# The exponential of the routing weights moved behind the key look-ups and behind a GELU; the turned keys copied by VectorE

## The chip, the cores and the metric

The kernel runs on one core of a Trainium2 chip. The metric is the time of one execution on the device, in microseconds (us). Five engines work side by side, each through its own queue, in the order of that queue: TensorE (PE in the profile; its weight loads are PEld), VectorE (DVE), ScalarE (ACT), GpSimd (POOL) and SyncE (SP, which here issues the loads). They meet only through waits that the program's builder puts on instructions.

## What is computed

A transformer forward pass over 256 tokens of width 1024, in float32: a first block (pooling, dilated attention, gates), and a second one with a convolution mixer and an attention mixer, each followed by an expert layer. The change is in the expert layer, which runs twice:

```python
def _peer(xn, w_q, subkeys, u_tab, v_tab):
    q = (t @ w_q).reshape(n_tok, PEER_HEADS, 2, SUB_DIM)           # 8 heads, 2 halves of a key
    sc = jnp.einsum("thpd,hpnd->thpn", q, subkeys)
    sv, si = lax.top_k(sc, PEER_TOPK)                              # the 16 best of 128 subkeys
    cand = sv[:, :, 0, :, None] + sv[:, :, 1, None, :]
    cidx = si[:, :, 0, :, None] * N_KEYS + si[:, :, 1, None, :]
    top_v, pos = lax.top_k(cand, PEER_TOPK)                        # the 16 best pairs
    idx = jnp.take_along_axis(cidx, pos, axis=-1)
    g = jax.nn.softmax(top_v, axis=-1)                             # the routing weights
    ...
    a = g * gelu(einsum(x, u_tab[idx]))
    out = einsum(a, v_tab[idx])
```

There are 128 x 128 experts. The kernel doesn't gather: it multiplies all tokens by all of U (128 tiles of 128 experts), takes the GELU, multiplies by the routing weights laid out over all experts, and multiplies by all of V.

## The kernel before

`peer` streams U tile by tile. For each of 128 tiles `i`: the tile comes by DMA in four buffers (L102); it is split into two parts of lower precision whose sum is exact, `hi` by ScalarE (L121) and `lo` by VectorE or GpSimd (L122; up to tile 41 always GpSimd), with three tiles in parts at a time; TensorE makes 24 products of it (L132 to L134) into one of two PSUM banks; ScalarE reads that bank with a GELU into `X` (L1138; L1134 for the tokens whose weights are there already). The bank is free for the tile after the next one only when its GELU is done.

Beside that the routing runs, cut into 36 jobs, traced over the first J1 = 40 tiles (job k ahead of tile k * 40 // 36). Four jobs end the lists of best subkeys (`lists`, L960 to L974). Then, for each half `a` of the tokens (128 each): `candidates` and `best` (L993 to L1015, the best 16 pairs of a head), one job with `ranks` (L1017 to L1039) and `weights` (L1055 to L1067), four `keys` jobs (L1041 to L1053: the subkeys at these ranks, each L1046, L1051, L1053), and `turn` (L1069 to L1078: three transposes on TensorE into one PSUM bank, of the two keys and the weights; then copies to SBUF as `ij` and, in two parts, `gt`). `weights` is the softmax: subtraction of the largest (L1058, VectorE), exponential (L1060, ScalarE), sum, reciprocal, scale and product (L1062 to L1065, VectorE). For the first half `ranks` and `weights` fall ahead of tile 15 and `turn` ahead of tile 21; for the second half ahead of tiles 33 and 38. From tile 40 on `scatter` (L1080 to L1104) lays the weights of four tokens at a time over all experts: VectorE makes `o` (L1084) and two `wi` (L1089) from `ij` and `gt`, TensorE multiplies them into `G` (L1094).

Most tiles of the routing (`g`, `tv`, `key0`, `key1`, `e`, `ra`, `rb`) have one buffer, which the second half's jobs take over from the first's: the second half's `key0` and `g` can be written when the first half's transposes have read theirs.

The order of each engine's queue isn't that of the text. A planner in the builder goes through the program with times of its own for each instruction; whenever an engine is free in its plan, it takes the earliest traced of those instructions whose inputs are there. The splits are raised in that order (`AHEAD`). What it fixed, the chip runs, whatever its real times. ScalarE's functions come in sets: the exponential and the GELU each need a table load (ACT_TABLE_LOAD) when the other was loaded; the casts and copies need none.

Of the kernel before, what the change touches and what calls it, by code (L numbers as in the profile page):

```python
# [22 lines left out]
# The tokens stand in the order of (t % 4, t // 4 % 4, t // 16), in which a query's keys of the  # L23
# dilations 4 and 16 lie in its own half.
ORDER = np.arange(T).reshape(16, 4, 4).transpose(2, 1, 0).reshape(T)
# a head of two in a tile, its half of the partitions, and the other half
# [4 lines left out]
G_SCALE = 16384.0      # the routing weights' two float16 parts carry float32's significand  # L31
# how far ahead of their place in the program: splits of streamed weights, of kept ones, the norms
AHEAD, KEEP, CHAIN = 200, 100, 4000
HL = 3                 # streamed tiles in two parts at a time
WARM = 14              # products that start TensorE's clock while the first tokens load
RELIEF = 3             # splits behind a norm that leave VectorE to it
# peer: the tiles of U over which the routing ends and over which its weights are scattered, the
# tiles of V whose products for the second tokens come last, the tiles of X in its first part
# [12 lines left out]
def two_blocks(ctx: ExitStack, tc: tile.TileContext, io, out):  # L51
# [10 lines left out]
    def as_ordered(ap):  # L62
        """[128, T] in the sequence's order, read or written in ORDER's, and the other way round."""
        return ap.rearrange("p (c i j) -> p j i c", i=4, j=4)
# [26 lines left out]
    count, relief, fetched, pin, pinned = [0], [0], [0], [None], [0]  # L91

    more = []

    def fetch(src):
        """One tile on its way; where a phase has more room, every third in that."""
        fetched[0] += 1
        if more and fetched[0] % 3 == 1:
            raw = more[-1].tile([P, D], F32, tag="more", name="more")
        else:  # L100
            raw = stream.tile([P, D], F32, tag="raw", name="raw", bufs=4)
        SY.dma_start(out=raw, in_=src)  # L102
        return raw
# [21 lines left out]
    def in_order(dst, src):  # L125
        """A load behind the ones that stand before it: it may have to wait for its place."""
        tc.keep_in_program_order(SY.dma_start(out=dst, in_=src))
# [8 lines left out]
    def dense_t(src, acts, pool_share=0):  # L136
        """[128 columns of W, 256 tokens] of (tokens @ W), in PSUM; src: [128, 8, 128]."""
# [7 lines left out]
    def stacked(ps, dst):  # L145
        """Two heads' queries, over 8, in two parts: each head's first part in its half of the
        partitions, and its second in the other half."""
# [9 lines left out]
    def keeper(pool, src):  # L157
        """keep(i): W's rows 128 i.. in their two parts, read once for both token tiles."""
# [11 lines left out]
    def rows_kept(act_of, keep, nxt):  # L170
        """x += the sum over 8 tiles of act[:, a]^T @ W's 128 rows: all of the first token tile, then
        all of the second beside the first one's next norm."""
# [19 lines left out]
    def last_rows(nxt, acc0, acc1, steps, scale=None):  # L192
        """The second token tile's last products, one half after the other, and around them the
        way from the first one's sums into the next layer."""
# [38 lines left out]
    def sum_squares(a, half, k=0, of=None):  # L233
        """64 * mean(x * x), one half of it."""
# [4 lines left out]
    def mean_square(a):  # L239
        """64 * (mean(x * x) + eps)."""  # L240
# [5 lines left out]
    def inverse_root(a, m):  # L246
        """1 / sqrt(m / 64): Newton's steps r -> r * (3 - m * r * r) / 2, where each step's factor
        of 2 goes into the next step's m (64 * m, 16 * m, 4 * m)."""
# [14 lines left out]
    def spread(pool, src, tag="spread"):  # L263
        """A row of D parameters on all partitions."""
# [5 lines left out]
    class Enter:  # L270
        """The norm in front of a layer, and the products of the layer's first 512 columns, which run
        token tile by token tile: the first tile's while the second's sums are still open.
        take(a, sums [128 tokens, 512]); new(shape, type, name): a tile."""
# [32 lines left out]
        def both(self, a, r):  # L306
            """added and scaled in one."""
# [34 lines left out]
        def open(self):  # L342
            """Room for the products until the next layer has turned them."""
# [4 lines left out]
    class EnterConv(Enter):  # L348
        """Behind the first block: its closing norm and the convolution's, in one."""
# [18 lines left out]
        def inverse(self, a):  # L368
            """Of both norms: 1 / sqrt(mean(y * y) + eps * (mean(x * x) + eps)) with y = x * gain."""
# [13 lines left out]
    def turned(nat, n, which=p_tr):  # L383
        """n transposes of [128, 128], side by side in PSUM."""
# [8 lines left out]
    def split_act(pool, src, tag, bufs=1):  # L393
        """An SBUF tile [128, n] in two float32r parts."""
# [7 lines left out]
    def transpose_p(pool, pieces, name, bufs=None, which=p_acc):  # L402
        """Transposes of [128, 128] pieces, side by side."""
# [13 lines left out]
    # ------------------------------------------------------------------ first block  # L417
    def first_block(nxt):
        acts = xh, xl
        with ExitStack() as es:  # L420
# [66 lines left out]
            def window(g):  # L487
                """Windowed means minus the value."""
# [102 lines left out]
    def attention(acts, es1, at1, v_n, att, rest, loads):  # L591
        """Softmax over the keys of all three groups together."""
# [3 lines left out]
        # the first group's: per head a query's two parts, and over both the keys' first part  # L596
# [108 lines left out]
    # ------------------------------------------------------------------ second block  # L705
# [54 lines left out]
    def gqa_mixer(entered, nxt):  # L760
        acts, nat = (xh, xl), entered.nat
        with ExitStack() as es:
# [11 lines left out]
            def place_keys():  # L774
                """Each key head twice, over the queries' two parts."""
# [19 lines left out]
            def place(i):  # L795
                """Two heads of one key head: tile pair, partition half, tile, head."""
# [34 lines left out]
            def weighted(i, p_ts, pv):  # L831
                """Both key heads of a tile pair, each in its half of the partitions."""
# [91 lines left out]
    def peer(l, entered, nxt):  # L924
        acts, nat = (xh, xl), entered.nat
        with ExitStack() as es:
            with ExitStack() as es1:
# [8 lines left out]
                def xs(i):  # L936
                    return X[i >= XA][:, i % XA]
# [5 lines left out]
                # in the place of X's last parts  # L943
# [16 lines left out]
                def lists(n):  # L960
                    """The 16 best subkeys of one half of a head."""
# [79 lines left out]
                def keys(a, side, part):  # L1041
                    """The subkeys at these ranks, four heads at a time."""
# [12 lines left out]
                def weights(a):  # L1055
                    tv = state["tv"]
                    g = one.tile([P, 8, 16], F32, tag="g", name="g")
                    V.tensor_tensor(out=g, in0=tv, in1=tv[:, :, 0:1].to_broadcast([P, 8, 16]),  # L1058
                                    op=OP.subtract)
                    S.activation(out=g, in_=g, func=AF.Exp)  # L1060
# [6 lines left out]
                    state["g"] = g  # L1067

                def turn(a):  # L1069
# [5 lines left out]
                    S.copy(out=ij[:, :, s], in_=ps[:, 0:2 * P].rearrange("p (c t) -> p c t", c=2))  # L1075
# [4 lines left out]
                def scatter(tg, done):  # L1080
                    """The weights of four tokens over all experts, [key 1, token, key 0]."""
# [25 lines left out]
                for a in range(2):  # L1107
# [3 lines left out]
                    jobs.append(lambda a=a: (ranks(a), weights(a)))  # L1111
                    jobs += [lambda a=a, s=s, p=p: keys(a, s, p) for s in range(2) for p in range(2)]
                    jobs.append(lambda a=a: turn(a))
# [6 lines left out]
                for i in range(P):  # L1120
# [16 lines left out]
                    if ready < 64:  # L1137
                        S.activation(out=xs(i)[:, ready:], in_=ps[:, ready:], func=AF.Gelu)  # L1138
# [42 lines left out]
    class Finish:  # L1181
        """The closing norm, from the last sums."""
# [48 lines left out]
def _bucket(rel, n_buckets, max_distance):  # L1231
    """T5 bucket of a relative position (a constant of the shapes)."""
# [11 lines left out]
def _layout(a):  # L1244
    f = np.float32

    def cols(w, n0, n1):
        """Tiles of 128 columns: [tile, 128 rows, row block, 128]."""
# [6 lines left out]
    def rows(w):  # L1255
        """Tiles of 512 columns: [tile, 4, 128 rows, row block, 512]."""
# [76 lines left out]
```

## Time and profile before

| | |
|---|---|
| time of a run, median of 3 (lowest to highest) | 2212.44 us (2206.22 to 2213.91) |
| span of the profiled execution, first to last instruction | 2210.8 us |
| TensorE, products | busy 2152.8 us, 97%, 14288 instructions |
| TensorE, weight loads | 1961.3 us, 89% |
| VectorE | 1569.8 us, 71% |
| ScalarE | 1074.3 us, 49% |
| GpSimd | 353.3 us, 16% |
| DMA | 373.94 MB, mean 169 GB/s |

Of the profiled execution the span is what is listed; what lies around it is in the times of the runs alone. Busy shares are means over the whole span. A wait is put down to the engine whose instruction ended it last. Line numbers are those of the kernel before. The first GELU of U's tiles starts at 449.4 us in the first expert layer and at 1409.7 us in the second.

### The profile page before, as it was taken

What the parts mean: (1) busy time and instruction counts of PE and PEld (TensorE: products, weight loads), DVE (VectorE), ACT (ScalarE), POOL (GpSimd) and SP (SyncE); (2) the same over time, 40 slices, a digit from 0 to 9 for tenths busy, and PEclk for the clock granted to TensorE, in tenths of its full rate; (3) what the DMA queues carried; (4) which work ended last, traced back from release to release, by engine and by line L of the source; (5) the groups of instructions that cost most, each with busy time, mean ns of one, the idle gap of its engine ahead of it and who ended that gap; (6) DMA issues with size and microseconds to landing.
All of it is one profiled execution on the core that took longest, in us unless ns stands there. A gap on an engine that the chain in (4) does not pass through costs nothing. (4 is left out here: it accounts for less than half of the span.)

```text
span 2210.8 us, 37689 instructions
## 1 busy us (share of the span) xinstructions
PE 2152.8 (97%) x14288; PEld 1961.3 (89%) x14288; DVE 1569.8 (71%) x3045; ACT 1074.3 (49%) x1975; POOL 353.3 (16%) x167
## 2 busy tenths in 40 slices
PE   8999999998999999999999999989999999999998
PEld 7999988998999999888888767989999999888887
DVE  4456777798577898555666686994788896565665
ACT  4556544344444444444455574444444444444454
POOL 3310101378300000000000232687000000000000
PEclk9999999999999999999999999999999999999999
DMA  6635746345544444665656652545444446556664
GB/s 245 209 124 175 236 130 195 115 153 159 166 144 152 144 145 153 190 192 191 192 194 201 214 180 71 159 144 180 144 145 151 144 144 190 191 191 191 192 193 139
DMA packets 104437, 373.94 MB, mean 169 GB/s; under 512 B 12096, under 2 KB 14144, under 8 KB 103744
## 3 DMA queue, kind: packets, MB, share of 16 engines
q1 hardware_dynamic: 103968, 371.01, 52.3%
q8 instruction: 112, 1.84, 0.3%
q14 instruction: 69, 0.57, 0.1%
q10 hardware_dynamic: 288, 0.52, 0.1%
HBM read 370.44 MB, written 1.05 MB: 168 GB/s over the span
## 5 line engine op out<-in xcount | busy, mean ns | idle before, releaser
L132 PE MATMUL mm<-xh,hi 128*128 128x256 f32 x2880 | 834.7, 290 | 21.8 <-ACT xa L1138 21.4
L133 PE MATMUL mm<-xl,hi 128*128 128x256 f32 x2880 | 817.7, 284 | 0.0
L134 PE MATMUL mm<-xh,lo 128*128 128x256 f32 x2880 | 817.1, 284 | 0.4 <-POOL lo L122 0.4
L121 ACT CAST hi<-raw 128x1024 fp32r<-128x1024 f32 x600 | 632.0, 1054 | 299.0 <-issue 138.8
L122 DVE TENSOR_TENSOR lo<-raw,hi 128x1024 fp32r<-128x1024 f32 x484 | 591.7, 1223 | 222.4 <-ACT hi L121 217.7
L132 PEld LDWEIGHTS mm<-xh,hi 128*128 128x128 f32 x2880 | 556.7, 193 | 24.7 <-ACT xa L1138 22.2
L133 PEld LDWEIGHTS mm<-xl,hi 128*128 128x128 f32 x2880 | 556.0, 193 | 0.3
L134 PEld LDWEIGHTS mm<-xh,lo 128*128 128x128 f32 x2880 | 554.6, 193 | 1.0 <-POOL lo L122 0.8
L1159 PE MATMUL acc<-hi,al 128*128 128x512 f32 x976 | 384.5, 394 | 0.0
L1159 PE MATMUL acc<-lo,ah 128*128 128x512 f32 x976 | 382.6, 392 | 0.0
L1159 PE MATMUL acc<-hi,ah 128*128 128x512 f32 x976 | 378.7, 388 | 0.0
L122 POOL TENSOR_TENSOR lo<-raw,hi 128x1024 fp32r<-128x1024 f32 x118 | 307.7, 2619 | 248.3 <-ACT hi L121 239.0
L1159 PEld LDWEIGHTS acc<-lo,ah 128*128 128x128 f32 x976 | 183.2, 188 | 42.8
L1159 PEld LDWEIGHTS acc<-hi,ah 128*128 128x128 f32 x976 | 183.2, 188 | 40.9
L1159 PEld LDWEIGHTS acc<-hi,al 128*128 128x128 f32 x976 | 183.5, 188 | 36.4
L1151 ACT CAST ah<-xa 128x256 fp32r<-128x256 f32 x200 | 81.3, 407 | 271.8 <-PE acc L1159 271.0
L1152 DVE TENSOR_TENSOR al<-xa,ah 128x256 fp32r<-128x256 f32 x200 | 84.9, 425 | 111.2 <-ACT ah L1151 111.2
L294 POOL TENSOR_TENSOR enl<-raw,enh 128x1024 fp32r<-128x1024 f32 x5 | 12.4, 2487 | 850.9 <-ACT enh L293 850.9
L1094 PE MATMUL G<-wi,o 128*128 128x128 f16 x1024 | 142.9, 296 | 0.0
L1084 DVE TENSOR_TENSOR o<-iota,ij 128x1024 f16<-128x1024 f16 x128 | 94.4, 739 | 58.7 <-PE G L1094 58.1
L1104 ACT COPY xa<-G 128x240 f32<-128x240 f32 (+22 forms) x92 | 35.4, 385 | 200.3 <-DVE xa L1101 153.5
L1101 DVE TENSOR_TENSOR xa<-G,xa 128x400 f32<-128x400 f32 (+31 forms) x128 | 111.8, 873 | 11.0 <-PE G L1094 11.0
(461 smaller groups left out, 2190.6 us busy)
## 6 DMA issues: line engine op xcount, KB each, us to landing
raw<-in_peer_u_dram SPq DMA_DIRECT2D x256, 512.0 KB, 3.5
raw<-in_peer_v_dram SPq DMA_DIRECT2D x256, 512.0 KB, 3.5
raw<-in_peer_w_q_dram SPq DMA_DIRECT2D x24, 512.0 KB, 3.7
raw<-in_conv_w_in_dram SPq DMA_DIRECT2D x20, 512.0 KB, 4.4
raw<-in_w_rest_dram SPq DMA_DIRECT2D x18, 512.0 KB, 3.6
raw<-in_w_qk_dram SPq DMA_DIRECT2D x16, 512.0 KB, 4.2
more<-in_w_rest_dram SPq DMA_DIRECT2D x10, 512.0 KB, 3.6
raw<-in_w_v_dram SPq DMA_DIRECT2D x8, 512.0 KB, 4.6
```

What stands on the lines that cost most here:

```text
L121: S.copy(out=hi, in_=raw)
L122: (G if on_pool else V).tensor_tensor(out=lo, in0=raw, in1=hi.bitcast(F32), op=OP.subtract)
L132: PE.matmul(out=ps, lhsT=ah, rhs=bh, start=first and i == 0, stop=False)
L133: PE.matmul(out=ps, lhsT=ah, rhs=bl, start=False, stop=False)
L134: PE.matmul(out=ps, lhsT=al, rhs=bh, start=False, stop=last and i == n - 1)
L1084: V.tensor_tensor(out=o, in0=iota_4.unsqueeze(1).to_broadcast([P, 2, P, 4]), in1=ij[:, :, s].unsqueeze(2).to_broadcast([P, 2, P, 4]), op=O ...
L1094: PE.matmul(out=ps[:, t], lhsT=o[:, 1, :, t], rhs=wi[i][:, :, t], start=i == 0, stop=i == 1)
L1101: V.tensor_tensor(out=dst[:, :, :old], in0=ps[:, :, i0:i0 + old], in1=dst[:, :, :old], op=OP.mult)
L1104: S.copy(out=dst[:, :, old:], in_=ps[:, :, i0 + old:i0 + n])
L1151: S.copy(out=act[0], in_=src)
L1152: V.tensor_tensor(out=act[1], in0=src, in1=act[0].bitcast(F32), op=OP.subtract)
L1159: PE.matmul(out=acc[a][half], lhsT=p[:, s], rhs=r[:, d], start=i == 0 and w == 0, stop=i == P - 1 and w == 2)
```

## The change

The softmax is cut in three. `shifted` (the subtraction alone) is traced ahead of `ranks`, in the same job. A new job `exponentials` comes behind the four `keys` jobs; with `issue_after` the exponential gets a place in ScalarE's queue behind the last GELU traced before it (an order, not a wait). A further job holds the rest, `weights`; then `turn`. That makes 40 jobs for 40 tiles: for the first half `shifted` and `ranks` stand ahead of tile 14, the exponential ahead of tile 19, `weights` ahead of 20, `turn` ahead of 21; for the second half at 32, 37, 38 and 39. In `turn` the copy of the two turned keys goes from ScalarE to VectorE. The GELU's instruction is kept in `state["gelu"]`. The rest of the diff removes comments and changes no instruction.

```diff
-                def weights(a):
+                def shifted(a):
                     tv = state["tv"]
-                    g = one.tile([P, 8, 16], F32, tag="g", name="g")
-                    V.tensor_tensor(out=g, in0=tv, in1=tv[:, :, 0:1].to_broadcast([P, 8, 16]),
+                    state["g"] = one.tile([P, 8, 16], F32, tag="g", name="g")
+                    V.tensor_tensor(out=state["g"], in0=tv, in1=tv[:, :, 0:1].to_broadcast([P, 8, 16]),
                                     op=OP.subtract)
-                    S.activation(out=g, in_=g, func=AF.Exp)
+
+                def exponentials():
+                    with tc.issue_after(state["gelu"]):
+                        S.activation(out=state["g"], in_=state["g"], func=AF.Exp)
+
+                def weights():
+                    g = state["g"]
                     z = one.tile([P, 8], F32, tag="gz", name="gz")
...
-                    state["g"] = g
...
-                    S.copy(out=ij[:, :, s], in_=ps[:, 0:2 * P].rearrange("p (c t) -> p c t", c=2))
+                    V.tensor_copy(out=ij[:, :, s], in_=ps[:, 0:2 * P].rearrange("p (c t) -> p c t", c=2))
...
-                    jobs.append(lambda a=a: (ranks(a), weights(a)))
+                    jobs.append(lambda a=a: (shifted(a), ranks(a)))
                     jobs += [lambda a=a, s=s, p=p: keys(a, s, p) for s in range(2) for p in range(2)]
+                    jobs.append(exponentials)
+                    jobs.append(weights)
                     jobs.append(lambda a=a: turn(a))
...
                     if ready < 64:
-                        S.activation(out=xs(i)[:, ready:], in_=ps[:, ready:], func=AF.Gelu)
+                        state["gelu"] = S.activation(out=xs(i)[:, ready:], in_=ps[:, ready:],
+                                                     func=AF.Gelu).ins
```

## Rows read from the trace of the kernel before

**Rows 1.** TensorE's waits (total us, times, longest), and the timeline at one's end.
```profile
PE mm L132 <- ACT xa L1138: 21.4, 4, 9.2
...
471.84 0.58 PE L132 MATMUL mm<-xh,hi 128*128 128x256 f32 x1 [3.27 <-ACT xa L1138]
```

**Rows 2.** Waits of the other engines, the whole span.
```profile
DVE gt L1077 <- ACT ij L1075: 56.9, 2, 28.6
...
ACT g L1060 <- DVE g L1058: 22.2, 4, 9.4
```

**Rows 3.** ScalarE's timeline, first layer: start, duration, operation, [idle before, releaser].
```profile
507.58 0.37 ACT L1138 ACTIVATE xa<-mm 128x256 f32<-128x256 f32 x1
...
513.33 0.38 ACT L1138 ACTIVATE xa<-mm 128x256 f32<-128x256 f32 x1
...
513.99 1.28 ACT L1060 ACT_TABLE_LOAD   x1
521.17 0.31 ACT L1060 ACTIVATE g<-g 128x128 f32<-128x128 f32 x1 [5.90 <-DVE g L1058]
521.39 1.03 ACT L121 CAST hi<-raw 128x1024 fp32r<-128x1024 f32 x1
522.43 1.28 ACT L1138 ACT_TABLE_LOAD   x1
523.73 0.38 ACT L1138 ACTIVATE xa<-mm 128x256 f32<-128x256 f32 x1
```

**Rows 4.** Busy us of PE, PEld, DVE, ACT, POOL; PEclk, DMA, GB/s; after three stalls.
```profile
471.84:478.01 6.17, 6.17 (x29) 6.17 (x30) 6.17 (x7) 1.98 (x3) 4.41 (x2) 0.50 0.42 104
...
1432.08:1438.00 5.92, 5.92 (x49) 5.92 (x50) 5.92 (x4) 2.50 (x4) 5.92 (x3) 1.00 0.37 100
1486.04:1491.77 5.73, 5.73 (x27) 5.73 (x28) 5.73 (x5) 1.54 (x3) 4.99 (x2) 0.50 0.28 94
```

**Rows 5.** TensorE's timeline: the first half's transposes of the keys, both layers.
```profile
512.25 0.38 PE L1074 MATMUL tr<-ident,key 128*128 128x128 f32 x2
...
1470.61 0.38 PE L1074 MATMUL tr<-ident,key 128*128 128x128 f32 x2
```

**Rows 6.** VectorE's timeline, first layer, around the second half's first look-ups.
```profile
513.45 0.22 DVE L1023 TENSOR_SCALAR t<-pos 128x128 uint32<-128x128 uint32 x1
513.58 2.43 DVE L1025 TENSOR_SCALAR m__6335<-pos 128x128 f32<-128x128 uint32 x1
...
518.39 1.23 DVE L1051 TENSOR_TENSOR e<-e,sif 128x1024 bf16<-128x1024 bf16 x1
519.72 1.22 DVE L1053 TENSOR_REDUCE key<-e 128x64 f32<-128x1024 bf16 x1
520.86 0.28 DVE L1058 TENSOR_TENSOR g<-tv 128x128 f32<-128x128 f32 x1
```

**Rows 7.** VectorE's groups, 468.6 to 520 us: count, busy us, mean ns, idle before.
```profile
L1051 DVE TENSOR_TENSOR e<-e,sif 128x1024 bf16<-128x1024 bf16 x5 | 14.0, 2803 | 0.0
```

**Rows 8.** VectorE's timeline, second layer.
```profile
1437.52 2.38 DVE L1064 TENSOR_SCALAR gz<-gz 128x8 f32<-128x8 f32 x1
...
1440.08 2.50 DVE L1065 TENSOR_TENSOR g<-g,gz 128x128 f32<-128x128 f32 x1
...
1480.27 1.23 DVE L1051 TENSOR_TENSOR e<-e,sif 128x1024 bf16<-128x1024 bf16 x1
```

**Rows 9.** Timelines of TensorE and VectorE, first layer: second half's transposes to first scatter.
```profile
569.88 0.27 PE L1074 MATMUL tr<-ident,g 128*128 128x128 f32 x1
...
571.42 0.29 DVE L1077 CAST gt<-tr 128x128 f16<-128x128 f32 x1 [28.33 <-ACT ij L1075]
...
573.72 0.74 DVE L1089 TENSOR_TENSOR wi<-o,gt 128x512 f16<-128x512 f16 x2
...
575.76 0.41 PE L1094 MATMUL G<-wi,o 128*128 128x128 f16 x2
```

## Prediction

> **What bounds the kernel now.** I read the table of busy shares first: TensorE 97%, no other engine over 71%. So the time is TensorE's own work plus what it loses, and an edit on ScalarE or VectorE counts only where TensorE waits for it. The waits of TensorE come next. By far the largest is "mm <- ACT xa L1138", 21.4 us in 4 waits, two in each layer [rows 1]: a product finds its PSUM bank still unread, because the GELU that reads it is late. The first wait of each layer takes 3.3 us (one is shown), the second layer's other one 9.2, which leaves 5.7 for the first layer's. ScalarE's own waits say why: 22.2 us in 4, the exponential L1060 waiting for VectorE's subtraction L1058 [rows 2]. ScalarE's timeline shows one of them whole [rows 3]: GELU of tile 20 at 513.33, table load at 513.99, the exponential only at 521.17, and behind it, in the same queue, a cast, the second table load and the GELU of tile 21 at 523.73.
>
> The stalls have a second price. In the stretches after three of the four the granted clock is 0.50, the lower level (1.2 GHz); after one it is 1.00 [rows 4]. Half of 6.2, 5.0 (not shown) and 5.7 us is lost there, 8.5 us: 3.1 of it after the first layer's first stall. The four stalls cost 21.4 + 8.5 = **29.9 us**.
>
> **What is removed.** After the change the subtraction is traced ahead of the ranks, and the exponential stands behind the GELU of the tile before its own place. The list of jobs grows from 36 to 40 for 40 tiles, one per tile: the first exponential follows the GELU of tile 18, `turn(0)` stays at tile 21, the second exponential follows tile 36, and `turn(1)` moves from tile 38 to 39. The first subtraction is what ended the first stall, at 471.84 [rows 1], and the GELU of tile 18 comes 36 us later, at 507.58 [rows 3]. The second ran at 520.86 [rows 6], and tile 36 lies 16 tiles of 2.9 us behind tile 20. So neither exponential waits for VectorE any more, and all 29.9 us go.
>
> **What takes its place.** The weights' chain (sum, reciprocal, scale, product: L1062 to L1065) now follows a late exponential, and the third transpose of `turn(0)` needs its result. TensorE's queue runs in order, so it will stand at that transpose until VectorE has done the chain. Two questions: when does TensorE arrive, and when VectorE?
>
> TensorE took these transposes at 512.25 and 1470.61 [rows 5]. Without the first stall of each layer (3.3 us, and in the first layer 3.1 us of clock) it arrives at **505.9** and **1467.3**.
>
> VectorE's queue is fixed in advance by a planner, which takes the earliest traced instruction that it believes ready. What it believed is read from the order [rows 6]: L1053 of the second tokens, which needs the first transpose alone, stands before L1058, which is traced earlier but needs the third. So in the plan VectorE had done L1051 of those look-ups and stood idle when the transposes came. On the chip L1053 started 7 us behind them, though TensorE itself had lost 6.4 us by then: VectorE was some 14 us behind the plan, or more, because the splits of GpSimd hold its look-ups. L1051 takes 2.80 us on average [rows 7], and 1.23 where GpSimd is idle [rows 6]. Over its five that alone is 7.9 us.
>
> In the plan 3 to 4 us lie between the first exponential's end (the GELU of tile 18, then 1.28 and 0.31 us) and the transposes behind tile 20. With VectorE idle for as long as that, the chain is queued **behind** everything that VectorE did before the transposes, up to that L1051. I take this end. The chain then runs when the real, late VectorE gets there:
> - First layer: L1051 ended at 519.62. Less 0.6 us, for the four chain instructions that no longer stand ahead of it; less 2.2 us, by which L1025 was held (2.43 us, and its neighbours of the same size 0.2) [rows 6], since a standing TensorE leaves GpSimd no splits to hold it with; plus 1.0 us for the chain, under 4 times the 0.28 us of L1058: 517.8. The wait is 517.8 - 505.9 = 11.9 us.
> - Second layer: L1051 ended at 1481.50 [rows 8]. Two of the chain instructions that leave were held there, 2.38 and 2.50 us: less 5.0, plus 1.0: 1477.5. The wait is 10.2 us.
>
> Both are longer than waits that already brought the lower clock, so 2 x 2.8 us for that, the mean of the three losses. Sum: 11.9 + 10.2 + 5.7 = **27.8 us**. Bounds: 12 us, if the chain comes right behind the start of the ranks, 6 us earlier in both layers [rows 6], less what is given back, and no clock is lost; 36 us, if nothing is given back (14.7 + 15.2) and the clock takes 3.1 us each.
>
> **The smaller parts.** The copy of the turned keys goes from ScalarE to VectorE. The nearest row there is L1077, 0.29 us for half as many columns [rows 9], so 0.3 to 0.5 us; VectorE has no splits in these tiles, so four of them hold up nothing but the scatter (below). The 56.9 us of "gt <- ACT ij" [rows 2] are no gain: that wait ended at 571.42, but the transposes had ended only at 570.15 [rows 9], so some 1.2 of 28 us were ScalarE's; for the rest VectorE had nothing to do that TensorE wanted.
>
> On the way to the first scatter the copy does stand. Transposes end at 570.15, the second `wi` at 574.46, and TensorE takes `G` at 575.76 [rows 9]. With `turn` one tile later TensorE arrives 5.6 - 2.9 = 2.7 us after the transposes, and VectorE takes 4.3 - 1.2 + 0.4 = 3.5 us. I take the difference, 0.7 us in each layer (0 to 1.5): **1.4 us**.
>
> ScalarE around the exponential: from one GELU's start to the next one's end some 4.6 us, by the durations of rows 3 (0.38, 1.28, 0.31, 1.03, 1.28, 0.38, a little overlapped). TensorE wants that bank 2 x 2.9 - 1.1 = 4.7 us after the first GELU's start, as GELU 20 began 1.1 us behind its tile's end. It just fits: nothing, or 0.3 us each if the cover goes.
>
> The cast ends at 522.42 and the table load starts at 522.43 [rows 3]. The Trainium skill's "ScalarE: Activation LUTs" (What ACT_TABLE_LOAD costs) speaks against a change that keeps the exponential between two GELUs: it counts each switch at the load's 1283 ns and a drain of about 1380 ns, and advises one set at a time. By it the second exponential of each layer would hold TensorE for 2 x 1.38 us, and the sum would be some 5 us higher. The row has the load and no drain, so my sum leaves it out.
>
> Total: -29.9 + 27.8 + 1.4 = **-0.7 us**. The profiled span, 2210.8 us, lies 1.6 us under the median of the runs; carried to that median, 2212.4, it gives **2211.7 us**, no difference that can be told. By the bounds, 2194 to 2222.
>
> **The rivals.**
> 1. *The chain is in time.* If VectorE was still among the `best` lists in the plan when the exponential ended, the chain stands before the ranks and both waits vanish: 2212.4 - 29.9 + 1.4 = 2184 us. For it: load, exponential and chain take 3 to 4 us and the change leaves two tiles, 5.8 us, so a VectorE on plan would do. Against: the order of L1053 and L1058 [rows 6].
> 2. *VectorE is held all the way* (slower). If GpSimd has splits left while TensorE stands, the 0.6, 2.2 and 5.0 us aren't given back, and two instructions of each chain are held for 2.2 us each as they were in the second layer [rows 8]: 7.8 + 8.9 = 16.7 us over the forecast, 2228 us. The kernel is slower from 1 us of this on, and by half a per cent from 12. Against: few tiles are in two parts at a time, so GpSimd soon stops.
> 3. *It doesn't do what it says*: the exponential still waits for VectorE, and nothing is saved, 2212 us. The subtraction would have to come 36 us later than now; I see no reason.
>
> **How the numbers follow.** Forecast 0.64, chain in time 0.22, held all the way 0.09, no effect 0.05. Half a per cent is 11 us, about what a measurement of this kernel can tell from no change. Of the forecast's share some 0.06 lies under 2201.4 (chain among the ranks). So faster by over 0.5%: 0.22 + 0.06 = 0.28; within: 0.58 + 0.05 = 0.63; slower: 0.09. The range takes in the forecast's 2194 to 2222 and the better part of the first rival: 2183 to 2222.
>
> **What would show it.** Right: "mm <- ACT xa L1138" gone from TensorE's waits; in its place the third transpose of `turn`, waiting for the product L1065, once in each layer, 8 to 15 us, with a clock of 0.50 behind it; L1062 to L1065 behind the first L1051 of the second tokens; no wait before L1060. Wrong: no wait at the transposes (rival 1), or L1062 ahead of the ranks in VectorE's order. A wait at `G` L1094 over 1.5 us would show the later `turn` mis-sized; one left at L1138, the cover of ScalarE.

## The result, and the profile after

The changed kernel takes **2224.15 us** (median of 4 runs, 2220.63 to 2229.05); the kernel before, run beside it, 2213.18 (4 runs). The ratio is 1.0052, with a 95% interval of [1.003, 1.0075]: slower by half a per cent. The forecast of 2211.7 us said no difference; the measured time lies 2 us above its range.

| | before | after |
|---|---|---|
| span of the profiled execution | 2210.8 us | 2218.9 us |
| TensorE, products busy | 2152.8 us | 2147.0 us |
| VectorE busy | 1569.8 us | 1566.2 us |
| first GELU of U's tiles to first `G`, first layer | 126.3 us | 132.7 us |
| the same, second layer | 128.3 us | 131.9 us |

The last two rows are the stage that the change touches (starts of these instructions in the traces). It became 10.0 us longer in both layers together; the span only 8.1, as stretches outside the stage happened to be shorter. In the new kernel the exponential is L1063, the weights' chain L1068 to L1071, the transposes L1079, the copy to `ij` L1080, the products into `G` L1099, the GELU L1145.

TensorE's waits in the changed kernel (total us, times, longest):

```profile
PE tr L1079 <- DVE g L1071: 27.4, 2, 13.8
...
PE tr L1079 <- DVE key L1053: 5.6, 2, 2.8
...
PE G L1099 <- DVE wi L1094: 2.0, 2, 1.0
```

The wait at the GELU's bank [rows 1] is gone. In its place TensorE stands 33.0 us at the transposes of the first half, twice in each layer. TensorE's timeline in the first layer shows both (the bracket is the idle time before, and what ended it):

```profile
505.91 0.27 PE L1079 MATMUL tr<-ident,key 128*128 128x128 f32 x1
508.98 0.47 PE L1079 MATMUL tr<-ident,key 128*128 128x128 f32 x1 [2.79 <-DVE key L1053]
523.09 0.48 PE L1079 MATMUL tr<-ident,g 128*128 128x128 f32 x1 [13.64 <-DVE g L1071]
```

VectorE's timeline of the same time shows the chain, queued behind the second half's first L1051:

```profile
520.84 1.23 DVE L1051 TENSOR_TENSOR e<-e,sif 128x1024 bf16<-128x1024 bf16 x1
521.99 0.28 DVE L1068 TENSOR_REDUCE gz<-g 128x8 f32<-128x128 f32 x1
...
522.74 0.29 DVE L1071 TENSOR_TENSOR g<-g,gz 128x128 f32<-128x128 f32 x1
522.95 1.21 DVE L1053 TENSOR_REDUCE key<-e 128x64 f32<-128x1024 bf16 x1
```

Busy us of PE, PEld, DVE, ACT and POOL, then the granted clock, the DMA share and GB/s, in the stall and behind it (first two rows: first layer; third: second layer, behind its stall):

```profile
508.40:523.10 14.70, 0.48 (x2) 0.20 (x3) 14.46 (x70) 0.00 (x0) 3.65 (x2) 0.50 0.29 99
523.10:528.90 5.80, 5.80 (x27) 5.80 (x28) 5.70 (x9) 0.35 (x1) 0.00 (x0) 0.50 0.00 0
...
1487.40:1491.50 4.10, 4.04 (x19) 4.04 (x20) 4.07 (x8) 0.00 (x0) 0.00 (x0) 0.51 0.00 0
```

Behind the stalls the clock is at its lower level (1.2 GHz) for 5.8 and 4.1 us of work; half of that, 2.9 and 2.0, is lost. And GpSimd is busy for only 3.65 of the 14.70 us of the first stall: a standing TensorE does leave it without splits.

### The profile page after: what moved, and what is told of

Read it like the earlier page. It is cut to its first block, busy times and chain, and to the rows that moved or that the text cites. A ratio compares the mean times of both kernels' runs of the same rounds, so it can differ in the third digit from the quotient of the medians.

```text
span 2218.9 us, 37685 instructions
## 1 busy us (share of the span) xinstructions
PE 2147.0 (97%) x14288; PEld 1956.5 (88%) x14288; DVE 1566.2 (71%) x3049; ACT 1073.8 (48%) x1971; POOL 351.3 (16%) x167
## 5 line engine op out<-in xcount | busy, mean ns | idle before, releaser
L1099 PE MATMUL G<-wi,o 128*128 128x128 f16 x1024 | 142.9, 296 | 2.1 <-DVE wi L1094 2.0
L1089 DVE TENSOR_TENSOR o<-iota,ij 128x1024 f16<-128x1024 f16 x128 | 88.4, 691 | 58.2 <-PE G L1099 57.4
```

The costliest lines, as they stand in the source:

```text
L1089: V.tensor_tensor(out=o, in0=iota_4.unsqueeze(1).to_broadcast([P, 2, P, 4]), in1=ij[:, :, s].unsqueeze(2).to_broadcast([P, 2, P, 4]), op=O ...
L1099: PE.matmul(out=ps[:, t], lhsT=o[:, 1, :, t], rhs=wi[i][:, :, t], start=i == 0, stop=i == 1)
```

## Where VectorE lost the time

The chain came at 523.0, not at 517.8. VectorE's trace shows why some 50 us earlier, at the first half's ranks. In the kernel before:

```profile
468.74 0.22 DVE L1020 TENSOR_SCALAR t<-pos 128x128 uint32<-128x128 uint32 x1
...
469.28 0.22 DVE L1025 TENSOR_SCALAR m__5650<-pos 128x128 f32<-128x128 uint32 x1
...
470.02 0.28 DVE L1033 TENSOR_TENSOR rb<-rb,m__5650 128x128 f32<-128x128 f32 x1
...
498.67 1.20 DVE L1053 TENSOR_REDUCE key<-e 128x64 f32<-128x1024 bf16 x1
```

In the changed kernel:

```profile
469.66 2.42 DVE L1020 TENSOR_SCALAR t<-pos 128x128 uint32<-128x128 uint32 x1
...
472.41 2.44 DVE L1025 TENSOR_SCALAR m__5620<-pos 128x128 f32<-128x128 uint32 x1
...
475.38 2.50 DVE L1033 TENSOR_TENSOR rb<-rb,m__5620 128x128 f32<-128x128 f32 x1
...
507.73 1.19 DVE L1053 TENSOR_REDUCE key<-e 128x64 f32<-128x1024 bf16 x1
```

The same instructions take 0.22 to 0.28 us before and 2.4 to 2.5 after. GpSimd's timelines tell the difference. Before, it was idle from 466.31 to 470.17, over most of the ranks, and waited for `hi`:

```profile
463.91 2.40 POOL L122 TENSOR_TENSOR lo<-raw,hi 128x1024 fp32r<-128x1024 f32 x1 [0.44 <-ACT hi L121]
470.17 6.08 POOL L122 TENSOR_TENSOR lo<-raw,hi 128x1024 fp32r<-128x1024 f32 x2 [3.86 <-ACT hi L121]
```

ScalarE's timeline of the kernel before says why `hi` was late:

```profile
464.13 1.28 ACT L1060 ACT_TABLE_LOAD   x1
468.85 0.31 ACT L1060 ACTIVATE g<-g 128x128 f32<-128x128 f32 x1 [3.44 <-DVE g L1058]
469.07 1.03 ACT L121 CAST hi<-raw 128x1024 fp32r<-128x1024 f32 x1
```

The cast that makes `hi` stood in ScalarE's queue behind the exponential, which waited for VectorE's subtraction. The same wait held up the GELU behind it, and so TensorE, which stood only from 468.57 to 471.84 [rows 1]: TensorE's stall and GpSimd's pause are two effects of ScalarE's wait.

After, no exponential stands there, and one split follows the other:

```profile
469.48 2.52 POOL L122 TENSOR_TENSOR lo<-raw,hi 128x1024 fp32r<-128x1024 f32 x1 [0.47 <-ACT hi L121]
472.36 2.41 POOL L122 TENSOR_TENSOR lo<-raw,hi 128x1024 fp32r<-128x1024 f32 x1 [0.36 <-ACT hi L121]
475.25 2.48 POOL L122 TENSOR_TENSOR lo<-raw,hi 128x1024 fp32r<-128x1024 f32 x1 [0.48 <-ACT hi L121]
```

Each held instruction starts within 0.2 us behind the start of a split and ends within 0.2 us of its end (472.41 + 2.44 = 474.85; 472.36 + 2.41 = 474.77). The Trainium skill's "SBUF — State Buffer" (Who interferes with whom) describes this as an exclusive lock: the engine that issues first has the shared port pair for its whole instruction, and the other stands. The rows agree, and so does its exception: it says that a reduction isn't held, and L1053 takes 1.19 to 1.22 us in all rows here. So the engines do meet outside the waits that the builder puts on instructions: the hold shows in the length of an instruction and not as a wait in front of it.

So the wait that the change removes had itself let VectorE through the ranks. Without it VectorE comes to the last L1053 of the first half's keys 9.1 us later (498.67, 507.73), behind TensorE's arrival at 505.9; that is also the unforeseen first wait of 2.8 us. The three held instructions make 6.6 us of it, and two of L997 beside them (1.50 and 2.56 us for 0.41 and 0.34) another 3.3; 0.8 is gained elsewhere. Then TensorE's stall frees VectorE: the ranks of the second half run unheld, and of the 9.1 us all but 2.4 are regained by the L1051 ahead of the chain (518.39 in [rows 6], 520.84 now). In the second layer the ranks are held in the same way (2.42, 2.44 and 2.50 us), and that L1051 comes at 1485.21 where [rows 8] has 1480.27: 1.0 us later within a stage that starts 4.0 us later.

This is a reading of two traces. The experiments test it. Two kinds of numbers stand for each: the ratio to the kernel before run beside it, and the two stages from the first GELU to the first `G`. Beside the kernels that ran once, the kernel before had medians of 2215.93 us (A, I) and 2214.38 us (B, C).

| kernel | time us | ratio, 95% interval | stages us |
|---|---|---|---|
| before (profiled first) | 2212.44 | | 126.3, 128.3 |
| after | 2224.15 | 1.0052 [1.003, 1.0075] | 132.7, 131.9 |
| A after, no splits on GpSimd | 2177.06 (one run) | | 111.7, 111.7 |
| B before, no splits on GpSimd | 2177.29 (one run) | | 112.2, 112.2 |
| C after, pause of three splits | 2206.55 (one run) | | 123.3, 122.8 |
| D first transposes later | 2204.76 | 0.9952 [0.9935, 0.9969] | 121.8, 122.7 |
| E chain first | 2212.26 | 0.9985 [0.9975, 0.9994] | 124.4, 123.7 |
| F both | 2193.91 | 0.9905 [0.9889, 0.9922] | 117.3, 117.3 |
| G second half only | 2198.20 | 0.9925 [0.9909, 0.9942] | 119.6, 118.9 |
| H first half only | 2220.38 | 1.0032 [1.0018, 1.0045] | 129.6, 130.5 |
| I copy back on ScalarE | 2230.16 (one run) | | 132.9, 132.6 |
| J as F, last splits on VectorE | 2189.35 | 0.9890 [0.987, 0.991] | 116.6, 116.2 |
| K as F, all splits on VectorE | 2187.01 | 0.9873 [0.9861, 0.9885] | (see K) |
| L after, all splits on VectorE | 2189.72 | 0.9894 [0.9873, 0.9915] | 114.9, 114.9 |
| M before, all splits on VectorE | 2189.31 | 0.9890 [0.9868, 0.9911] | 115.8, 114.9 |

## Experiments: GpSimd's splits as the cause

**A. The changed kernel without GpSimd's splits** of U's first 42 tiles: the first part stands for the second in the products.

```diff
+        if pool_share == 1:
+            S.copy(out=hi, in_=raw)
+            return hi, hi
```

> The changed kernel without GpSimd's subtractions in the routing's tiles (the first 42 of U in both layers): hi stands in the place of lo in the products, as many of them as before; the output is therefore less exact. It asks how much of VectorE's lateness is GpSimd's. Theory: all. L1051 and L1046 take 1.2 us each everywhere, VectorE ends the chain about 20 us earlier, before TensorE arrives at 505.9, and the waits at L1079 go though the chain's place in the queue is the same; about 2185 us. Rival, the chain's place in the queue alone makes the wait (the backlog of the best lists is VectorE's own): half of it or more stays, 8 us in each layer, about 2200.

TensorE has no wait left in the stage; the chain keeps its place behind the second half's first look-up (L1051, here L1054) and ends at 502.5, before TensorE takes the last transpose at 504.2. VectorE's work in the stage, unheld (busy us of PE, PEld, DVE, ACT, POOL; clock):

```profile
447.60:559.30 111.70, 111.70 (x934) 111.67 (x932) 63.06 (x234) 56.80 (x84) 0.00 (x0) 1.00 0.56 181
```

The place of the chain alone costs nothing; a VectorE held by GpSimd makes it costly. That TensorE waited for the splits themselves is ruled out: none of its waits in the changed kernel is for GpSimd's `lo`.

**B. The kernel before without them**: the same three lines.

> The kernel before without GpSimd's subtractions in the routing's tiles (hi in the place of lo, output less exact). Theory: the stalls of the kernel before have the same cause as those of the changed one, VectorE late by GpSimd's holds against the plan; without holds the exponential finds its subtraction done or nearly, and the 21.4 us at L1138 fall under 6 us: about 2180 us, within 5 us of the changed kernel without splits. Rival, the exponential's place in ScalarE's queue makes these stalls by itself: over 12 us stay.

No wait in the stage either, 112.2 us: the stalls of the kernel before had the same cause, and without it the change is worth 0.5 us in a stage (one run of each).

**C. A pause of GpSimd at the ranks**: the changed kernel, but the splits of tiles 10 to 12 are left out (the first part stands for the second).

```diff
+    bare = [False]
...
+        if bare[0]:
+            S.copy(out=hi, in_=raw)
+            return hi, hi
...
+                    bare[0] = 10 <= i <= 12
```

> The changed kernel with GpSimd's subtraction left out for three tiles of U in each layer, 10 to 12, which it does while VectorE works on the first half's ranks (hi stands for lo in their products; the output is less exact). My prediction missed the wait at the transposes by 11 us: I took VectorE's ranks at the pace of the kernel before, where TensorE stood just then and GpSimd had run out of splits. In the changed kernel three instructions of the ranks are held, 2.4 to 2.5 us instead of 0.2. Theory: give the pause back and the chain comes 6 to 8 us earlier in each layer; the waits at L1079 go from 33 to 17 to 21 us in all. Rival, holds elsewhere make up for it (GpSimd is then ahead and holds later ones): the waits stay over 28 us.

```profile
PE tr L1083 <- DVE g L1075: 15.6, 2, 7.8
```

This is the only wait left at these transposes: 33.0 us become 15.6, rather more of a gain than I expected. The ranks run at 0.21 to 0.28 us each again, and the chain ends at 513.2 instead of 523.0. Three splits left out of 42, at the place where the removed wait had left a gap, take away over half of the wait.

## Experiments: the chain's place and TensorE's arrival

**D. The first half's transposes later**: `turn(0)` goes from tile 21 to 29, VectorE's order stays.

```diff
-                    jobs.append(lambda a=a: turn(a))
+                    if a:
+                        jobs.append(lambda: turn(1))
+                jobs.insert(29, lambda: turn(0))
```

> The changed kernel, with one job moved: turn(0), the first half's transposes, is traced at tile 29 instead of 21, behind most of the second half's best lists. VectorE's queue keeps its order up to the scatter; only TensorE takes the transposes 8 tiles (23 us) later. My theory: the changed kernel loses its time because TensorE reaches the transposes 16 us before VectorE has done the weights' chain. Then here it arrives at 505.9 + 23 = 529 us, behind the chain (523 to 526): the waits at L1079 (27.4 + 5.6 us) go to under 3 us in all, the lower clock behind them goes, and with the old stalls gone too the time is 25 to 32 us under the kernel before, 0.985 to 0.989 of it. Rival, VectorE's lateness itself costs the time and only changes its place: the second half's look-ups, which wait for the transposes, start 6 us later than in the changed kernel, and TensorE waits as long at the second transposes or at the first scatter; then it stays within 0.5% of the changed kernel, 1.005 of the one before.

TensorE's wait, and the chain's product in VectorE's timeline (first layer):

```profile
PE tr L1079 <- DVE g L1071: 11.6, 2, 5.8
...
535.47 0.29 DVE L1071 TENSOR_TENSOR g<-g,gz 128x128 f32<-128x128 f32 x1
```

Faster than before, but a wait of 5.8 us stays in each layer. Moving TensorE's arrival doesn't leave VectorE's time as it was: without the stall GpSimd goes on splitting, and the chain ends at 535.8, 12.7 us later than in the changed kernel. Of eight tiles' time more than half is eaten up so. It is the same mistake as in the prediction, made again in the expectation.

**E. The chain first**: the second half's `candidates(1, 1)`, and with it the look-ups behind, is tied to follow the chain's product in VectorE's queue.

```diff
+                    state["w"] = V.tensor_tensor(out=g, in0=g, op=OP.mult,
+                                                 in1=z.unsqueeze(2).to_broadcast([P, 8, 16])).ins
...
+                def behind_weights(job):
+                    with tc.issue_after(state["w"]):
+                        job()
...
+                        cand = lambda a=a, part=part: candidates(a, part)
+                        jobs.append((lambda c=cand: behind_weights(c)) if a and part else cand)
```

> The changed kernel, with the second half's last candidates and with them what needs them (four best lists, the ranks, the first look-ups) tied behind the weights' product in VectorE's queue. So the chain stands behind the first half's look-ups, not behind the second half's first ones. Theory: what counts is where the chain stands in VectorE's queue. VectorE ends the first half's look-ups at 508.9, 3.0 us after TensorE's arrival; then comes the rest of a few best lists, a cast and the chain, about 3 us: waits of 5 to 8 us in each layer in place of 16.4, half of them perhaps without the lower clock; 17 to 24 us less than the changed kernel, 0.994 to 0.998 of the one before. Rival, TensorE waits for the exponential or a later step and not for the chain's place: the waits stay at 16 us each and the time at 1.005.

```profile
PE tr L1083 <- DVE g L1071: 8.3, 2, 4.2
PE tr L1083 <- DVE key L1053: 5.6, 2, 2.8
```

The waits are as expected, the gain is a little smaller: the chain ends at 514.1, 9 us sooner, and of 33.0 us 13.9 stay. The waits at the second key are unchanged: that part is VectorE's lateness, not the chain's place.

**F. Both**: chain first, and `turn(0)` at tile 26.

> The changed kernel with both: the weights' chain tied ahead of the second half's last candidates in VectorE's queue, and turn(0) at tile 26 instead of 21 (arrival about 520 us). In turn_late the chain itself had come 13 us later, at 535.7, because a TensorE that doesn't stall leaves GpSimd its splits and VectorE is held for all of the backlog ahead of the chain. Theory: the wait is arrival against chain, and VectorE's pace while nothing stalls is the slow one. Here the chain follows the first half's look-ups (508 to 510), a few lists and a cast, with holds 515 to 519: no wait at the first transposes. All old stalls are gone: 22 to 29 us under the kernel before, 0.987 to 0.990 of it; what could be left is a wait of up to 4 us in each layer at the second transposes, as the routing fills VectorE up to about 558 us. Rival, VectorE's whole work up to the scatter is too long and the wait only moves to the second transposes or the scatter with its full size: 8 us or more in each layer there, 0.994 to 0.997.

```profile
PE mm L134 <- POOL lo L122: 2.9, 14, 0.2
...
PE tr L1083 <- DVE g L1071: 2.4, 2, 1.2
```

Faster than both kernels, by 1% than the one before, just short of what I expected. The transposes of the first half wait for nothing; at those of the second half 1.2 us a layer are left. Most of the rest of the stage (117.3 against 111.7 us) lies in its last part, where TensorE now waits for GpSimd. The stage by engine (as for A):

```profile
451.20:568.50 117.30, 114.46 (x935) 112.33 (x934) 112.30 (x235) 57.01 (x85) 108.17 (x39) 1.00 0.56 173
```

VectorE is busy 112.30 of 117.30 us and GpSimd 108.17. Against A, 39 splits on GpSimd cost VectorE 112.30 - 63.06 = 49.2 us, **1.26 us each**.

## Experiments: which part of the change

**G. The second half's exponential alone** is moved and tied; the first half's weights stand with its ranks as before.

```diff
-                def exponentials():
+                def exponentials(tied=False):
+                    if not tied:
+                        S.activation(out=state["g"], in_=state["g"], func=AF.Exp)
+                        return
...
-                    jobs.append(lambda a=a: (shifted(a), ranks(a)))
+                    if a:
+                        jobs.append(lambda a=a: (shifted(a), ranks(a)))
+                    else:
+                        jobs.append(lambda a=a: (ranks(a), shifted(a), exponentials(), weights()))
...
```

> Half of the change: the first half's weights as in the kernel before (exponential behind the ranks, not tied), the second half's as in the changed kernel; the copy on VectorE. Theory: the first half's exponential is what costs (its chain lands behind VectorE's backlog, 33 us and the lower clock), the second half's is what gains (5.7 and 9.2 us of waits and 5.4 us of clock). Then TensorE waits 3.3 us in each layer for the GELU behind the first exponential and not at the transposes nor for the second exponential: 15 to 21 us under the kernel before, 0.990 to 0.994. Rival, either half costs as much as it gains: 0.998 to 1.003.

```profile
PE mm L132 <- ACT xa L1152: 6.5, 2, 3.3
```

As expected: the first stall of each layer stays, and with it GpSimd's pause (in the first layer 3.86 us for `hi`, up to 470.76); the first half's ranks run at 0.22 to 0.28 us each. The second stall goes, and at the transposes TensorE waits once, for 0.7 us.

**H. The first half's exponential alone**: the two conditions of G turned round.

> Edit: in the changed kernel only the first half's exponential is moved and tied; the second half's weights stand with its ranks as in the kernel before. Theory (what the first half's later chain costs is a stall in which VectorE catches up): the two waits at the first half's transposes stay at about 16 us a layer, but in them VectorE runs without GpSimd's splits and reaches the second half's subtraction while TensorE still stands, so the second exponential's stall (9.2 and 5.7 us before) shrinks to 0 to 3 us a layer. About the changed kernel's time: ratio to before 1.000 to 1.006. Rival (the stalls are independent): both stand, 33 us at the transposes and 15 us at the GELU's bank and half clock behind them: ratio 1.010 to 1.016.

```profile
PE tr L1082 <- DVE g L1074: 30.8, 2, 15.4
```

The theory held: the first half's ranks are held again (2.43, 2.44 and 2.50 us), TensorE waits 15.4 us a layer at the transposes, and not at the GELU's bank, though the second exponential was not moved. The stalls are not independent. ScalarE still waits 16.2 us a layer for the second half's subtraction, but nearly all of it lies within TensorE's own stand at the transposes (in the first layer 512.2 to 528.4 against 511.1 to 526.5), so the bank is read in time.

**I. The copy to `ij` back on ScalarE.**

```diff
-                    V.tensor_copy(out=ij[:, :, s], in_=ps[:, 0:2 * P].rearrange("p (c t) -> p c t", c=2))
+                    S.copy(out=ij[:, :, s], in_=ps[:, 0:2 * P].rearrange("p (c t) -> p c t", c=2))
```

> The changed kernel with one part undone: the copy of the turned keys on ScalarE again. Theory: this part costs and brings next to nothing; the waits at the first transposes stay at 16 us in each layer, and the way to the first scatter gets 0.8 us longer (1.2 less 0.4), so the wait at G goes from 1.0 to about 1.8 us in each layer: 2 us more in all, less than one run can tell. Rival, the copy on VectorE is what holds the queue: the waits at L1079 shrink by more than 2 us.

The waits at the transposes are the same, 27.4 and 5.6 us; those at `G` grew from 2.0 to 2.8 us in all, less than expected. The copy has no part in the waits that make the result. The single time is 6 us above the changed kernel's median; 0.9 us of that lie in the two stages, and where the rest comes from stays open.

## Experiments: the plan and the load

The planner puts each instruction where VectorE would be free for it by its own times. If its error is GpSimd's holds, then splits that VectorE makes itself, 1.22 us each, load VectorE as much as the held ones, but stand in the plan.

**J. As F, with the splits of tiles 38 to 41 on VectorE.**

```diff
-                    ps = dense_t(io["peer_u"][l, i], acts, int(i < J1 + 2)).rearrange(
+                    ps = dense_t(io["peer_u"][l, i], acts, int(i < J1 - 2)).rearrange(
```

> Edit: the version with the chain tied first and the first transposes at tile 26, and the splits of U's tiles 38 to 41 on VectorE. What is left in that version against the kernels without GpSimd's splits is 5.6 us in a layer (117.3 against 111.7 us from the first GELU to the first G). Theory: GpSimd is the bound of that stage's last part: its splits take 3.38 us there while a tile of TensorE takes 2.9, and TensorE waits 0.2 us at each for the part lo. Four splits fewer give 2 us a layer back, and VectorE loses nothing, as a split costs it 1.22 us itself and 1.26 us when GpSimd holds it (112.3 less 63.1 us busy, over 39 splits): ratio to before 0.988 to 0.990. Rival: VectorE's queue comes to these splits late, behind the look-ups, and TensorE waits for them: 0.992 to 0.997.

```profile
PE mm L134 <- POOL lo L122: 1.9, 9, 0.2
PE mm L134 <- DVE lo L122: 1.6, 1, 1.6
```

In the expected band; but a stage got 0.9 us shorter where 2 were expected: in the first layer TensorE still waits seven times for GpSimd, 1.4 us in all, and in the second one split of VectorE's was itself late. Against F the difference is within the intervals.

**K. As F, with all of these splits on VectorE** (0 for the last argument).

> Edit: the same version with all of U's first 42 splits on VectorE, none on GpSimd. Theory (a split of GpSimd's costs VectorE as much time as VectorE's own would): VectorE's busy time in the stage is 63.1 + 39 x 1.22 = 110.7 us, where it is 112.3 with GpSimd's splits; the stage is 112 to 118 us long and the ratio to before 0.986 to 0.992. Rival (the hold is cheap and GpSimd's help is real): VectorE's queue, in order, brings the splits late, TensorE waits for them 10 us or more in each layer, and the ratio is above 1.00.

The lowest ratio, 0.9873; its interval lies below F's, but not below those of J, L and M. The granted clock of its profiled execution was 0.94 on average, where the others here have 0.98 or more, so its length of the stage isn't compared. The stage by engine:

```profile
457.50:571.60 114.10, 113.19 (x943) 112.86 (x942) 108.77 (x300) 57.60 (x84) 0.00 (x0) 0.95 0.56 177
```

VectorE's busy time is 108.77 us, 2 us under the 110.7 that I worked out, and less than F's 112.30 with GpSimd's help; one of its own splits takes 1.22 us here as elsewhere. The help was worth nothing.

**L. The changed kernel with all of them on VectorE**, nothing else changed.

> Edit: the changed kernel with all of U's first 42 splits on VectorE, and nothing else. The planner then counts VectorE's whole load; in its order the chain L1068 to L1071 stands ahead of the second half's look-ups, where with GpSimd's splits it stands behind their first L1051. Theory (the order was wrong because the plan knew nothing of what GpSimd's splits cost VectorE): VectorE is about on plan, TensorE waits under 3 us in each layer at the first half's transposes, and the ratio to before is 0.985 to 0.991. Rival (VectorE, 110 us of 112 busy, is late for the transposes wherever the chain stands): waits of 8 us or more in each layer, ratio 0.994 to 1.003.

```profile
PE tr L1079 <- DVE g L1071: 3.7, 2, 1.9
```

The first stage by engine, here and in the changed kernel (as for A):

```profile
447.00:561.90 114.90, 113.06 (x943) 112.78 (x943) 108.95 (x300) 57.68 (x85) 0.00 (x0) 1.00 0.57 176
...
449.20:581.90 132.70, 115.34 (x935) 114.54 (x934) 96.03 (x235) 57.77 (x86) 102.17 (x39) 0.92 0.51 153
```

33.0 us of waits become 3.7. In the queue the chain stands ahead of the second half's look-ups now. VectorE doesn't have less to do: it is busy for 108.95 us of the 114.90 of this stage, and for 96.03 of 132.70 in the changed kernel. Its load is larger, and in the plan.

**M. The kernel before with all of them on VectorE.**

> Edit: the kernel before with all of U's first 42 splits on VectorE, and nothing else. Theory (the stalls at the GELU's bank come from a VectorE that is behind a plan which doesn't count GpSimd's holds): they fall from 21.4 us to under 6 with the moved splits alone, and the ratio to before is 0.986 to 0.992, within 0.3% of the changed kernel with the same splits. Rival (the exponential waits in ScalarE's queue wherever VectorE is full): 15 us or more stay, ratio 0.995 to 1.003.

```profile
PE mm L132 <- ACT xa L1138: 4.5, 3, 2.0
```

21.4 us become 4.5. L and M are the same, 0.9894 and 0.9890: where the plan has VectorE's whole load, the change makes no difference that these runs can tell. Both of its effects, the stalls that it removes and the ones that it brings, need GpSimd's holds (A, B). That the plan leaves these holds out is inferred from its order; a plan that counts them, with the splits still on GpSimd, was not tried.

## Why the prediction was wrong

- **What is removed: right.** No wait is left at the GELU's bank, and ScalarE goes from GELU to load to exponential without a gap:

```profile
501.00 0.37 ACT L1145 ACTIVATE xa<-mm 128x256 f32<-128x256 f32 x1
501.39 1.28 ACT L1063 ACT_TABLE_LOAD   x1
502.68 0.31 ACT L1063 ACTIVATE g<-g 128x128 f32<-128x128 f32 x1
502.92 1.05 ACT L121 CAST hi<-raw 128x1024 fp32r<-128x1024 f32 x1
503.98 1.28 ACT L1145 ACT_TABLE_LOAD   x1
```

  No time is lost around either load: the drain that the Trainium skill's "ScalarE: Activation LUTs" (What ACT_TABLE_LOAD costs) adds to each switch isn't there, and leaving it out of the sum was right.
- **TensorE's arrival: right.** 505.91 for 505.9; in the second layer 1470.29 for 1467.3 + 4.0 of shift, 1.0 early.
- **The chain's place: right**, behind the second half's first L1051; and its length, 1.04 us for 1.0.
- **VectorE's time: the step that failed.** "Less 0.6 us ..., less 2.2 us", and 5.0 in the second layer, took VectorE's times from the trace of before and subtracted what the new stall gives back. It left out what the exponential's old wait had given: ScalarE, standing there, left GpSimd without `hi`, and so VectorE without holds. Without that wait VectorE is held through the first half's ranks and is 9.1 us late in the first layer before the new stall begins. The L1051 ahead of the chain was forecast 2.8 and 5.0 us earlier than before; it came 2.4 later and 1.0 later. The waits are 16.4 and 16.6 us for 11.9 and 10.2: **33.0 for 22.1**. No bound covered this: the upper one, 14.7 + 15.2, assumed that nothing is given back, which is to say that VectorE is as late as before, never later.
- **The clock**: 4.9 us for 5.7. **`G`**: 2.0 us for 1.4, with the copy at 0.42 us in the forecast 0.3 to 0.5. **ScalarE's cover**: nothing, as taken.
- **The sum**: -29.9 + 33.0 + 4.9 + 2.0 = +10.0 us, which is what the two stages grew by. Of the sum's error of 10.7 us the waits make 10.9, `G` 0.6 and the clock -0.8.
- **The rivals.** That the chain is in time (2184 us) is what A shows without the holds; on the chip as it stands it didn't happen. "VectorE is held all the way" had the sign and the engine, not the place: its "against" was right, GpSimd made two splits in a stall of 14.7 us. The holds came before the stall, where the prediction didn't look, since the trace of before has none there. 0.09 for slower was too little for a sum in which a stall of 27.8 us replaces one of 29.9.

## What to carry to other kernels

A wait that is removed has been idle time for other engines, here for GpSimd through one cast in ScalarE's queue: before taking a second engine's times from the old trace, ask what ran free during the wait and what will hold it when the wait is gone, and follow that engine again from there to the next meeting point. An order fixed by a plan is only as good as the plan's durations: where two engines hold each other, the load that the plan doesn't count shows as instructions of one size with two durations, and moving work to the engine that pays for it anyway can cost nothing and mend the plan. When two moves are tried together, try each alone: here one was worth 0.75% and the other cost 0.3%.

## What the runs showed of the hardware

A split of [128, 1024] on GpSimd took 2.4 us where VectorE ran small instructions and 3.38 beside the look-ups (537.8 to 557.9 us in F), and cost VectorE 1.26 us on average; VectorE's own split takes 1.22 us (mean of 484 in the changed kernel). I had not expected the exchange to be so even that GpSimd's help is worth nothing in a stage that fills VectorE. The granted clock was at 0.50 over 14.7 us of the first layer's stall and for 5.8 us of work behind it, where [rows 4] had 6.2 us behind a stall of 3.3: a stall four times as long did not cost more clock.
